# Products with the low parts of the weights moved to the end of each granule

## The chip, the cores and the metric

The kernel runs on one core of a Trainium2 chip. The metric is the device time of one execution in microseconds (us). A profile of one execution stands beside it: the span from the first to the last instruction, and what each engine did in it.

TensorE (PE in the profile) multiplies, VectorE is DVE, ScalarE is ACT, GpSimd is POOL, and SP is the queue that issues most transfers. Each engine works through its own queue in order and waits on semaphores where an operand comes from another engine.

## The reference, cut to what matters

One layer of a decoder trunk with 512 tokens and 2048 channels, all in float32:

```
h    = rmsnorm(x) * (1 + scale) + shift
proj = h @ w_in          # 2048 x 13632
q_lat, kv_lat, k_rope, z_mla, u, v, z_sgu, g_mla, g_sgu = split(proj)
y_mla  = causal_attention(q_lat, kv_lat, k_rope) * silu(z_mla)
y_sgu  = u * (tril(w_spatial) @ rmsnorm(v) + b_spatial) * silu(z_sgu)
merged = sigmoid(g_mla) * y_mla + sigmoid(g_sgu) * y_sgu
out    = rmsnorm(x + gate * (merged @ w_out))
```

The change lies in the projection `h @ w_in`, which takes the greater part of the time.

## The kernel before, in words

**Products in three parts.** A float32 operand is split into a high part (a cast to fp32r) and a low part (the rest). A product of two such operands is three matmuls added up in one PSUM bank: high by high, high by low, low by high. `mm3` (L156 to L159) issues these three in a row.

**Granules.** Weights arrive in granules of 128 rows and up to 1024 columns. For each granule ACT casts the high part (`w0h`, `w1h`, `Xh`), and DVE subtracts it from the raw tile to give the low part (`w0l`, `w1l`, `Xl`). The low part is therefore always ready after the high part. Which of the tiles a granule uses goes in turns: two pairs (`w0`, `w1`) in the stages before the blocks, three (`w1`, `w0`, `X`) in the blocks. A cast into a pair must wait until TensorE has read the high part of the granule that had the pair before, and a subtraction until it has read the low part.

**Stages.** The first stage (L440 to L464) projects 1024 columns into eight banks. The second stage (`ps2`, L524 to L536) projects 640 columns into five banks `ps2`: sixteen granules `g2[j]`, each of five `mm3`, 15 matmuls of 512 tokens. The plain stage (L704 to L732) has sixteen granules `gb[st]` and five banks `plain[0..4]` in the same way; in the granules 2, 5, 8, 11, 14 and 15 it adds matmuls for the rotary key (L720, L721). Beside its matmuls TensorE's neighbours have other work there: DVE sums the modulation weights, corrects `hh` and `hl` (the parts of h), and makes the sums of h's quarters; `lat_out` (L512) copies the five finished banks out on ACT at the start of the plain stage, and `evac_plain` (L622, L626) does so for `plain`.

**Blocks.** The remaining columns are done in eleven blocks of seven quarter products (a Strassen-like scheme), each block in 28 granules and each granule in 12 matmuls (L1440 to L1450): for each of two rows of channels `k` and two token halves `t` (bank `ps[t]`), the three parts of a product. 11 x 28 x 12 = 3696 matmuls. In the blocks the weights are the moving operand. Around the matmuls of granule s the lists of events run in a fixed order on ACT and DVE (`run(s, FIRST, HIGH, EVAC, GATE, SPLIT, BACK)`): HIGH casts the high part for granule s+2, EVAC copies out or combines banks that the granule before has finished, SPLIT makes the low part for granule s+2.

**After the blocks.** The attention projections (`mm_low_last`, L1541 to L1552) and the output projection (`out_granule`, L1749 to L1764) already issue all matmuls with the high part of the weights first and those with the low part last.

The order within every queue is as written in the program (`manual_schedule`); nothing reorders it.

Of the kernel before, what the change touches and what calls it, by code (L numbers as in the profile page):

```python
# [20 lines left out]
P = 128  # L21
D = 2048
S = 512
KC = D // P
# [113 lines left out]
def trunk_layer(ctx, tc, xT, xn, c, vecs, pos, wada, w1, w2, wv, wv3, wv4, wh, wh15, wq, wqr, wk, wvv, wo, wsT, bsp, gfin, out,  # L138
                dbg=None):
    nc = tc.nc  # L140
    ACT, DVE, PE, DMA = nc.scalar, nc.vector, nc.tensor, nc.sync
    LEFT, RIGHT = "left", "right"

    def tt(out, in0, in1, op):
        DVE.tensor_tensor(out=out, in0=in0, in1=in1, op=op)  # L145
# [10 lines left out]
    def mm3(ps, ah, al, bh, bl, start, stop):  # L156
        PE.matmul(ps, ah, bh, start=start, stop=False)  # L157
        PE.matmul(ps, ah, bl, start=False, stop=False)  # L158
        PE.matmul(ps, al, bh, start=False, stop=stop)  # L159
# [18 lines left out]
    def nt(p, shape, dt, tag, **kw):  # L178
        uid[0] += 1
        return p.tile(shape, dt, tag=tag, name=f"{tag}_{uid[0]}", **kw)  # L180
# [152 lines left out]
    def get(i, ahead=1, run=1):  # L333
        r = ws.get(i, ahead)
        fs, pend[:] = pend[:run], pend[run:]
        for f in fs:
            f()
        return r
# [8 lines left out]
    def bank_at(k):  # L347
        return nt(psp.p, [P, S], F32, f"ps{k}")

    def bank():  # L350
        n_bank[0] += 1
        return bank_at(ring[(n_bank[0] - 1) % len(ring)])
# [54 lines left out]
    hh, hl = [None] * KC, [None] * KC  # L407
# [21 lines left out]
    for q in range(4):  # L429
        for r in range(per):  # L430
            sl = slice(r * (S // per), (r + 1) * (S // per))
# [10 lines left out]
    for j in range(KC):  # L442
# [4 lines left out]
        wH, wL = get(g1[j], ahead=0)  # L447
# [11 lines left out]
        cols = [slice(m * P, (m + 1) * P) for m in range(8)]  # L459
# [6 lines left out]
                mm3(ps1[m], wH[:, cols[m]], wL[:, cols[m]], hh[j], hl[j], False, j == KC - 1)  # L466
    tt(ssx, ssx, sq, ALU.add)

    n_dot = 0

    def dot_to(n):
        nonlocal n_dot
        while n_dot < min(n, KC):
            ada_dot(n_dot)
            n_dot += 1
# [3 lines left out]
    def fix_begin(s_):  # L479
        if s_ in FIX_AT:  # L480
            j0 = n_fix
            assert n_dot >= j0 + 2
            tt(shift[:, j0:j0 + 2], dots[:, j0:j0 + 2], vec[:, C_BADA + j0:C_BADA + j0 + 2], ALU.add)
            tt(tw, xw[j0 // 2], rx.unsqueeze(1).broadcast_to([P, 2, S]), ALU.mult)

    def fix_end(s_):

        nonlocal n_fix
        if s_ in FIX_AT:
            js = low_at[s_ + 1] = range(n_fix, n_fix + 2)  # L490
# [12 lines left out]
    def store(dst, src):  # L503
        made.append((dst, src))

    def stores(n=None):
        for dst, src in leaving[:n]:
            DMA.dma_start(dst, src)
        leaving[:], made[:] = (leaving[n:] if n else []) + made, []
# [13 lines left out]
    ps2 = [bank() for _ in range(5)]  # L523
    for j in range(KC):  # L524
        fix_begin(j)
        wH, wL = get(g2[j])
        for m in range(5):
            sl = slice(m * P, (m + 1) * P)
            mm3(ps2[m], wH[:, sl], wL[:, sl], hh[j], hl[j], j == 0, j == KC - 1)
        if j < NB:  # L530
            DVE.reciprocal(out=rx[:, j * P:(j + 1) * P], in_=rx[:, j * P:(j + 1) * P])
        fix_end(j)
        dot_to(DOTS[j])
        if j == NB - 1:
            store(rx_d, rx)
        if j >= NB - 1:  # L536
            stores(1)
# [164 lines left out]
    plain = []  # L702
    for st in range(KC):
        fix_begin(KC + st)  # L704
        if st == 0:
            for f in pend:
                f()
            pend.clear()
        wH, wL = get(gb[st], ahead=0 if st == KC - 1 else 1)
        fix_end(KC + st)  # L710
        if KC + st < len(DOTS):
            dot_to(DOTS[KC + st])
        if st == 0:
            plain += [bank_at(k) for k in (3, 4, 5, 6, 7, 0)]
        for m in range(5):
            sl = slice(m * P, (m + 1) * P)
            mm3(plain[m], wH[:, sl], wL[:, sl], hh[st], hl[st], st == 0, st == KC - 1)
        for i, k in enumerate(rope_in.get(st, ())):
            both = wH[:, (5 + i) * P:(6 + i) * P]
            PE.matmul(plain[5], both, hh[k], start=k == 0, stop=False)  # L720
            PE.matmul(plain[5], both, hl[k], start=False, stop=k == KC - 1)  # L721
        if st == SUMS_AT:
            assert n_fix == KC
            ada.close()
            s12 = Scope("s12")
            for n in ("s2", "s1"):
                sums[n] = nt(s12.p, [P, 8, 2, 256], F32R, n)
            tb = Scope("tB")
        for f in early.pop(st, ()):
            f()  # L730
        stores(1)
# [547 lines left out]
    for group in (((10, "lat8"), (11, "lat9")), ((12, "lat10"), ("plain", "sinT"))):  # L1279
# [9 lines left out]
        i = group[0][0]  # L1289
# [126 lines left out]
    for b in range(len(BLOCKS)):  # L1416
        if b == 1:
            ring[:], n_bank[0] = [5, 6], 0
        for g, (p, i) in enumerate(V7):
            s = done[0] = at_block[b] + g  # L1420
            n = 1 if b or g else 2
            for f in pend[:n]:
                f()
            del pend[:n]
            for f in early.pop(KC + g, ()):
                f()
            if (b, g) == (1, 4):
                assert not pend and not early
                tb.close()
                mis = Scope("more")  # L1430
                sg[0] = Scope("sgu")
            if (b, g) == (1, 6):
                wide.clear()
            if g == 0 and b:
                v7["y_before"] = v7["y"]
            run(s, FIRST, HIGH, EVAC, GATE, SPLIT, BACK)
            if i == 0 and p in (1, 5, 6):
                which, banks = {1: ("y", y_of[b % 2]), 6: ("z", z_of), 5: ("w", z_of if b else (5, 6))}[p]
                v7[which] = [bank_at(k) for k in banks]
            ps = v7["y" if p < 5 else "z" if p > 5 else "w"]  # L1440
            wH, wL = (w.rearrange("p (k h w) -> p k h w" if BLOCKS[b][0] == "v" else "p (h k w) -> p k h w", h=4, k=2)
                      for w in vparts.pop((b, g)))
            for k in range(2):
                xh, xl = rights[p](2 * i + k)
                st, sp = i == k == 0 and p in (1, 5, 6), i == 3 and k == 1
                for t in range(2):
                    tk = slice(t * P, (t + 1) * P)
                    PE.matmul(ps[t].rearrange("p (h w) -> p h w", h=4), xh[:, tk], wH[:, k], start=st, stop=False, skip_group_check=True)  # L1448
                    PE.matmul(ps[t].rearrange("p (h w) -> p h w", h=4), xl[:, tk], wH[:, k], start=False, stop=False, skip_group_check=True)  # L1449
                    PE.matmul(ps[t].rearrange("p (h w) -> p h w", h=4), xh[:, tk], wL[:, k], start=False, stop=sp, skip_group_check=True)  # L1450
            run(s, MISC, LOAD)
            stores()
    v7["y_before"] = v7["y"]
# [133 lines left out]
    def kproj(h, ahead=1):  # L1587
        wH, wL = get(gk[h], ahead)
        ps = bank()
        mm_low_last(ps, wH, wL, range(6, 10))  # L1590
        return ps
# [154 lines left out]
    ps = kproj(0, 0)  # L1746
# [114 lines left out]
    for cg, k in ((2, 1), (3, 4)):  # L1861
        st = chunk_at[4 * cg + 3] + 1
# [21 lines left out]
    for cg in range(4):  # L1884
        for n in range(NB):
            cols = slice(cg * S, (cg + 1) * S)
# [131 lines left out]
```

## Time and profile before

| what | value |
|---|---|
| median of 3 runs | 1542.17 us (1541.4 to 1545.81) |
| the profiled execution: its time | 1543.22 us |
| the profiled execution: its span | 1541.3 us |
| PE busy | 1524.6 us, 99% of the span, 7152 matmuls |
| DVE busy | 1234.3 us, 80% |
| ACT busy | 806.6 us, 52% |
| POOL busy | 169.2 us, 11% |
| DMA, mean | 219 GB/s |
| granted TensorE clock, mean | 0.997 |

The time is 1.9 us more than the span, for what lies around it. A matmul that is shown with 0.39 us is pipelined: what counts for the rate is the distance from one start to the next, about 0.227 us for 512 columns. TensorE has waited where that distance is longer, and the bracket at the end of such a row names what ended the wait.

### The profile page before, as it was taken

The numbers are of one execution on the slowest core, as the hardware profiler recorded it, in microseconds if no ns is written. First come the engines' busy times: TensorE is split into PE (matmuls) and PEld (weight loads), VectorE is DVE, ScalarE is ACT, GpSimd is POOL, SyncE is SP. The second block draws the span as 40 slices with busy tenths as digits, with TensorE's granted clock in tenths as the row PEclk, the third lists the DMA queues.
The fourth block names the chain that finished last, engine by engine and source line by source line (L and its number), as shares of the span: only waits on it lengthen the run. The fifth ranks groups of instructions, "written<-read, shape, count | busy, mean of one in ns | idle before, by whom it ended". The sixth has DMA issues, their size and how long they took to land.

```text
span 1541.3 us, 20555 instructions
## 1 busy us (share of the span) xinstructions
PE 1524.6 (99%) x7152; PEld 1273.6 (83%) x7152; DVE 1234.3 (80%) x1676; ACT 806.6 (52%) x1276; POOL 169.2 (11%) x161
## 2 busy tenths in 40 slices
PE   9999999999999999999999999999999999999997
PEld 7888878888888887888888888888788888888886
DVE  8989897768787888887888787878689889965753
ACT  4445555546555546454555555556666666532331
POOL 0000000101000000011010100000122223221120
PEclk9999999999999999999999999999999999999999
DMA  9979775858886786878776866777788877759732
GB/s 377 388 269 347 237 220 164 233 148 241 245 223 184 214 227 199 226 214 212 206 200 186 223 205 190 236 193 215 193 205 195 203 185 193 194 148 338 283 103 110
DMA packets 368922, 337.93 MB, mean 219 GB/s; under 512 B 133689, under 2 KB 313969, under 8 KB 363697
## 3 DMA queue, kind: packets, MB, share of 16 engines
q1 hardware_dynamic: 345906, 313.54, 65.3%
q0 software_dynamic: 22912, 23.07, 9.7%
q8 instruction: 56, 0.92, 0.2%
q14 instruction: 48, 0.39, 0.1%
HBM read 302.38 MB, written 34.17 MB: 218 GB/s over the span
## 4 chain that ended last, share of the span: by engine, by line
PE 90%; DVE 4%; DMA 2%; SPq 2%; ACT 1%; issue 1%; ACTq 0%; DVEq 0%
PE ps L1448 17%; PE ps L1450 17%; PE ps L1449 17%; PE ps L463 5%; PE ps L158 5%; PE ps L159 5%; PE ps L157 5%; PE ps L1761 3%; PE ps L1763 3%; PE ps L1764 3%; PE ps L1549 3%; PE ps L1550 2%; PE ps L1552 2%; PE ps L1632 1%; SPq L102 1%
## 5 line engine op out<-in xcount | busy, mean ns | idle before, releaser
L145 DVE TENSOR_TENSOR X<-X,X 128x1024 fp32r<-128x1024 f32 (+2 forms) x111 | 130.4, 1182 | 28.8 <-ACT X L688 27.3
L688 ACT CAST X<-X 128x1024 fp32r<-128x1024 f32 x70 | 73.7, 1053 | 96.4 <-PE ps L1449 58.9
L688 ACT CAST w0h<-X 128x1024 fp32r<-128x1024 f32 x70 | 73.7, 1053 | 95.2 <-PE ps L1449 47.0
L688 ACT CAST w1h<-X 128x1024 fp32r<-128x1024 f32 x69 | 72.6, 1052 | 80.0 <-PE ps L1449 41.6
L145 DVE TENSOR_TENSOR w0l<-X,w0h 128x1024 fp32r<-128x1024 f32 x70 | 85.5, 1221 | 30.5 <-ACT w0h L688 28.9
L145 DVE TENSOR_TENSOR w1l<-X,w1h 128x1024 fp32r<-128x1024 f32 x69 | 84.2, 1221 | 25.7 <-ACT w1h L688 25.7
L122 DVE TENSOR_TENSOR w0l<-wraw,w0h 128x1024 fp32r<-128x1024 f32 (+3 forms) x61 | 65.7, 1078 | 36.3 <-ACT w0h L121 20.4
L145 DVE TENSOR_TENSOR X<-wraw,X 128x1024 f32<-128x1024 f32 (+1 forms) x65 | 79.3, 1221 | 16.9 <-ACT X L688 15.1
L122 DVE TENSOR_TENSOR w1l<-wraw,w1h 128x1024 fp32r<-128x1024 f32 (+3 forms) x60 | 69.9, 1165 | 28.6 <-ACT w1h L121 21.1
L1450 PE MATMUL ps<-w0l,hh 128*128 128x512 f32 x236 | 92.0, 390 | 0.4 <-DVE w0l L145 0.4
L1449 PE MATMUL ps<-w0h,hl 128*128 128x512 f32 x236 | 91.9, 389 | 0.0
L1450 PE MATMUL ps<-w1l,hh 128*128 128x512 f32 x236 | 91.8, 389 | 0.0
L1449 PE MATMUL ps<-w1h,hl 128*128 128x512 f32 x236 | 91.8, 389 | 0.0
L1448 PE MATMUL ps<-w0h,hh 128*128 128x512 f32 x236 | 91.8, 389 | 0.0
L1448 PE MATMUL ps<-w1h,hh 128*128 128x512 f32 x236 | 91.8, 389 | 0.0
L121 ACT CAST w0h<-wraw 128x1024 fp32r<-128x1024 f32 (+3 forms) x61 | 52.8, 866 | 73.1 <-PE ps L1764 20.4
L1450 PE MATMUL ps<-X,hh 128*128 128x512 f32 x232 | 90.6, 391 | 0.4 <-DVE X L145 0.4
L1448 PE MATMUL ps<-X,hh 128*128 128x512 f32 x232 | 90.4, 390 | 0.0
L1449 PE MATMUL ps<-X,hl 128*128 128x512 f32 x232 | 90.3, 389 | 0.0
L148 DVE SCALAR_TENSOR_TENSOR wada<-wada,cact 128x2048 f32<-128x2048 f32 x39 | 88.9, 2281 | 0.7 <-DMA wada<-in_wada 0.7
L121 ACT CAST w1h<-wraw 128x1024 fp32r<-128x1024 f32 (+3 forms) x60 | 52.6, 877 | 61.9 <-PE ps L158 20.1
L145 DVE TENSOR_TENSOR wraw<-wraw,X 128x1024 f32<-128x1024 f32 x66 | 80.4, 1218 | 0.6 <-DMA X<-in_wh 0.6
(462 smaller groups left out, 4404.2 us busy)
## 6 DMA issues: line engine op xcount, KB each, us to landing
X<-in_wh SPq DMA_DIRECT2D x131, 512.0 KB, 5.2
wada<-in_wada SPq DMA_DIRECT2D x39, 1024.0 KB, 7.6
wraw<-in_wo SPq DMA_DIRECT2D x32, 512.0 KB, 4.5
wraw<-in_wh SPq DMA_DIRECT2D x21, 512.0 KB, 5.1
wraw<-in_wh POOLq DMA_DIRECT2D x21, 512.0 KB, 7.7
turned<-p_d SPq DMA_DIRECT2D x64, 160.0 KB, 3.9
X<-in_wv SPq DMA_DIRECT2D x17, 512.0 KB, 4.1
X<-in_wh SPq DMA_DIRECT2D x22, 384.0 KB, 5.3
```

Source lines behind the costliest of these rows:

```text
L121: self.nc.scalar.copy(hi[:, :n], raw[:, :n])
L122: self.nc.vector.tensor_tensor(out=lo[:, :n], in0=raw[:, :n], in1=hi[:, :n].bitcast(F32), op=ALU.subtract)
L145: DVE.tensor_tensor(out=out, in0=in0, in1=in1, op=op)
L148: DVE.scalar_tensor_tensor(out=out, in0=in0, scalar=scalar, in1=in1, op0=op0, op1=op1, **kw)
L157: PE.matmul(ps, ah, bh, start=start, stop=False)
L158: PE.matmul(ps, ah, bl, start=False, stop=False)
L159: PE.matmul(ps, al, bh, start=False, stop=stop)
L463: PE.matmul(ps1[m], a[:, cols[m]], b, start=(j == 0 and a is wH and b is hh[j]), stop=False)
L688: ACT.copy(hi, t)
L1448: PE.matmul(ps[t].rearrange("p (h w) -> p h w", h=4), xh[:, tk], wH[:, k], start=st, stop=False, skip_group_check=True)
L1449: PE.matmul(ps[t].rearrange("p (h w) -> p h w", h=4), xl[:, tk], wH[:, k], start=False, stop=False, skip_group_check=True)
L1450: PE.matmul(ps[t].rearrange("p (h w) -> p h w", h=4), xh[:, tk], wL[:, k], start=False, stop=sp, skip_group_check=True)
```

## The change

A new function `low_last` issues for one granule first the two matmuls with the high part of the weights for every bank, and then the one with the low part for every bank. The second and the plain stage call it in place of five `mm3`. In the blocks the loop over k and t runs twice, first for the high part and then for the low part. Number, size and operands of the matmuls stay the same.

```
+    def low_last(banks, wH, wL, k):
+        cols = [slice(m * P, (m + 1) * P) for m in range(len(banks))]
+        for m, ps in enumerate(banks):
+            PE.matmul(ps, wH[:, cols[m]], hh[k], start=k == 0, stop=False)
+            PE.matmul(ps, wH[:, cols[m]], hl[k], start=False, stop=False)
+        for m, ps in enumerate(banks):
+            PE.matmul(ps, wL[:, cols[m]], hh[k], start=False, stop=k == KC - 1)
...
-        for m in range(5):
-            sl = slice(m * P, (m + 1) * P)
-            mm3(ps2[m], wH[:, sl], wL[:, sl], hh[j], hl[j], j == 0, j == KC - 1)
+        low_last(ps2, wH, wL, j)
...
-            mm3(plain[m], wH[:, sl], wL[:, sl], hh[st], hl[st], st == 0, st == KC - 1)
+        low_last(plain[:5], wH, wL, st)
...
+            for low in (False, True):
+                for k in range(2):
...
+                        if low:
+                            PE.matmul(to, xh[:, tk], wL[:, k], start=False, stop=sp, skip_group_check=True)
+                        else:
+                            PE.matmul(to, xh[:, tk], wH[:, k], start=st, stop=False, skip_group_check=True)
+                            PE.matmul(to, xl[:, tk], wH[:, k], start=False, stop=False, skip_group_check=True)
```

In the rows below a name is a tile with its running numbers: `ps` a bank, `w0h`/`w0l` and `w1h`/`w1l` the high and low part of a granule, `hh`/`hl` those of h. On PE, the last rows of the plain stage's granule 11 ahead of its rotary matmuls, before:

```order
L158 MATMUL ps_144_1470<-hl_138_1391,w1h_1593 128x512
L159 MATMUL ps_144_1470<-hh_135_1360,w1l_1594 128x512
L157 MATMUL ps_145_1471<-hh_135_1360,w1h_1593 128x512
L158 MATMUL ps_145_1471<-hl_138_1391,w1h_1593 128x512
L159 MATMUL ps_145_1471<-hh_135_1360,w1l_1594 128x512
L157 MATMUL ps_146_1472<-hh_135_1360,w1h_1593 128x512
L158 MATMUL ps_146_1472<-hl_138_1391,w1h_1593 128x512
L159 MATMUL ps_146_1472<-hh_135_1360,w1l_1594 128x512
```

The same rows of PE's queue now:

```order
L472 MATMUL ps_145_1471<-hh_135_1360,w1h_1593 128x512
L473 MATMUL ps_145_1471<-hl_138_1391,w1h_1593 128x512
L472 MATMUL ps_146_1472<-hh_135_1360,w1h_1593 128x512
L473 MATMUL ps_146_1472<-hl_138_1391,w1h_1593 128x512
L475 MATMUL ps_142_1468<-hh_135_1360,w1l_1594 128x512
L475 MATMUL ps_143_1469<-hh_135_1360,w1l_1594 128x512
L475 MATMUL ps_144_1470<-hh_135_1360,w1l_1594 128x512
L475 MATMUL ps_145_1471<-hh_135_1360,w1l_1594 128x512
L475 MATMUL ps_146_1472<-hh_135_1360,w1l_1594 128x512
```

The first use of `w1l` moved from the 3rd to the 11th matmul of the granule, the last use of `w1h` for the five banks from the 14th to the 10th (the rotary matmuls behind them still read it), and the bank `ps_142` is finished by the 11th instead of the 3rd.

On PE, the first eleven matmuls of the first block's granule 4 (counted from 0), with the waits that they carry, before:

```order
L1448 MATMUL ps_190_2035<-w0h_2081,hh_134_1357 128x512 [waits Activation_49]
L1449 MATMUL ps_190_2035<-w0h_2081,hl_137_1389 128x512
L1450 MATMUL ps_190_2035<-w0l_2082,hh_134_1357 128x512 [waits DVE_49]
L1448 MATMUL ps_191_2036<-w0h_2081,hh_134_1357 128x512
L1449 MATMUL ps_191_2036<-w0h_2081,hl_137_1389 128x512
L1450 MATMUL ps_191_2036<-w0l_2082,hh_134_1357 128x512
L1448 MATMUL ps_190_2035<-w0h_2081,hh_135_1360 128x512
L1449 MATMUL ps_190_2035<-w0h_2081,hl_138_1391 128x512
L1450 MATMUL ps_190_2035<-w0l_2082,hh_135_1360 128x512
L1448 MATMUL ps_191_2036<-w0h_2081,hh_135_1360 128x512
L1449 MATMUL ps_191_2036<-w0h_2081,hl_138_1391 128x512
```

The same eleven matmuls' places now:

```order
L1457 MATMUL ps_190_2035<-w0h_2081,hh_134_1357 128x512 [waits Activation_49]
L1458 MATMUL ps_190_2035<-w0h_2081,hl_137_1389 128x512
L1457 MATMUL ps_191_2036<-w0h_2081,hh_134_1357 128x512
L1458 MATMUL ps_191_2036<-w0h_2081,hl_137_1389 128x512
L1457 MATMUL ps_190_2035<-w0h_2081,hh_135_1360 128x512
L1458 MATMUL ps_190_2035<-w0h_2081,hl_138_1391 128x512
L1457 MATMUL ps_191_2036<-w0h_2081,hh_135_1360 128x512
L1458 MATMUL ps_191_2036<-w0h_2081,hl_138_1391 128x512
L1455 MATMUL ps_190_2035<-w0l_2082,hh_134_1357 128x512 [waits DVE_49]
L1455 MATMUL ps_191_2036<-w0l_2082,hh_134_1357 128x512
L1455 MATMUL ps_190_2035<-w0l_2082,hh_135_1360 128x512
```

The wait for DVE's low part moved from the 3rd to the 9th matmul. The high part is read for the last time by the 8th instead of the 11th, and the bank of the first token half is finished by the 11th instead of the 9th.

On ACT, two casts and the copies of the two banks behind them in a later block (`d` is the tile that holds a copied quarter), before:

```order
L688 CAST w1h_2759<-X_250_2443 128x1024 [waits DMASW4_49,DMASW5_49,PE_49,Activation_49]
L688 CAST w0h_2781<-X_289_2660 128x1024 [waits DMAHW5_49,DMAHW6_49,DVE_49,PE_49]
L906 COPY d_310_2784<-ps_282_2623 128x512
L906 COPY d_310_2784<-ps_283_2624 128x512 [waits PE_49]
L688 CAST X_311_2800<-wraw_260_2491 128x1024 [waits DMASW6_49,DMASW7_49,DVE_49,PE_49]
```

The same rows now:

```order
L694 CAST w1h_2759<-X_250_2443 128x1024 [waits DMASW4_49,DMASW5_49,PE_49,Activation_49]
L694 CAST w0h_2781<-X_289_2660 128x1024 [waits DMAHW5_49,DMAHW6_49,DVE_49,PE_49]
L910 COPY d_310_2784<-ps_282_2623 128x512 [waits PE_49]
L910 COPY d_310_2784<-ps_283_2624 128x512 [waits PE_49]
L694 CAST X_311_2800<-wraw_260_2491 128x1024 [waits DMASW6_49,DMASW7_49,DVE_49,PE_49]
```

The queue is in the same order; the copy of the first bank has a wait for PE of its own, since the wait of the cast ahead of it no longer covers the bank's last matmul. There are 43 such copies on ACT. The queues of DVE, POOL and SP are the same as before, with the same engines waited for.

More of the change, by code (lines that the diff above doesn't have):

```diff
@@ L714, in trunk_layer @@
             plain += [bank_at(k) for k in (3, 4, 5, 6, 7, 0)]
-        for m in range(5):
-            sl = slice(m * P, (m + 1) * P)
-            mm3(plain[m], wH[:, sl], wL[:, sl], hh[st], hl[st], st == 0, st == KC - 1)
+        low_last(plain[:5], wH, wL, st)
         for i, k in enumerate(rope_in.get(st, ())):
@@ L1442, in trunk_layer @@
                       for w in vparts.pop((b, g)))
[L1443 to L1450, printed above, removed]
+            for low in (False, True):
+                for k in range(2):
+                    xh, xl = rights[p](2 * i + k)
+                    st, sp = i == k == 0 and p in (1, 5, 6), i == 3 and k == 1
+                    for t in range(2):
+                        tk = slice(t * P, (t + 1) * P)
+                        to = ps[t].rearrange("p (h w) -> p h w", h=4)
+                        if low:
[3 more added lines that the diff above has]
+                            PE.matmul(to, xl[:, tk], wH[:, k], start=False, stop=False, skip_group_check=True)
             run(s, MISC, LOAD)
```

## The prediction

> **What bounds the kernel now.** I read the page's engine totals, the chain that ended last, the stages, and then every distance between two starts of matmuls, since a busy share of 99% does not tell how often TensorE waits.
>
> ```profile
> PE 1524.6 (99%) x7152; PEld 1273.6 (83%) x7152; DVE 1234.3 (80%) x1676; ACT 806.6 (52%) x1276; POOL 169.2 (11%) x161
> PE 90%; DVE 4%; DMA 2%; SPq 2%; ACT 1%; issue 1%; ACTq 0%; DVEq 0%
> 98.00:152.00 54.00, 54.00 (x239) 44.50 (x237) 46.86 (x55) 23.44 (x34) 0.00 (x0) 1.00 0.94 346
> 152.00:217.00 65.00, 63.48 (x278) 51.65 (x277) 56.57 (x95) 34.95 (x56) 0.00 (x0) 1.00 0.76 236
> 217.00:1075.00 858.00, 856.85 (x3780) 705.74 (x3779) 698.68 (x795) 471.53 (x612) 68.01 (x56) 1.00 0.75 208
> 1345.00:1492.00 147.00, 147.00 (x689) 123.12 (x688) 92.72 (x114) 46.39 (x73) 27.57 (x22) 1.00 0.70 231
> ```
>
> The rows by stage give the stretch, its length, and the busy time of PE, PEld, DVE, ACT and POOL, then the granted clock. PE's idle time is 0.00 us in the second stage, 65.00 - 63.48 = 1.52 in the plain stage, and 858.00 - 856.85 = 1.15 in the eleven blocks. An order of matmuls can win only what TensorE waits in these 977 us, some 3 us.
>
> Does the order itself have a price? Two granules of a block (old order) and the starts of two output granules (high first, low last):
>
> ```profile
> 700.43 0.39 PE L1448 MATMUL ps<-w1h,hh 128*128 128x512 f32 x1
> 703.15 0.39 PE L1448 MATMUL ps<-w0h,s 128*128 128x512 f32 x1
> 1409.99 1.81 PE ps L1761 x8
> 1415.43 1.81 PE ps L1761 x8
> ```
>
> Old: (703.15 - 700.43) / 12 = 0.2267 us from start to start. New pattern: (1415.43 - 1409.99) / 24 = 0.2267 us. The 480 reordered matmuls of the two stages and the 3696 of the blocks cost the same either way, at a granted clock of 1.00 in both stages' rows.
>
> **The change part by part.** *1. The waits for the low part go.* These are the places where the third matmul of a granule came late (its row behind the second's):
>
> ```profile
> 187.81 0.39 PE L158 MATMUL ps<-hl,w1h 128*128 128x512 f32 x1
> 188.47 0.50 PE L159 MATMUL ps<-hh,w1l 128*128 128x512 f32 x1 [0.27 <-DVE w1l L122]
> 195.44 0.39 PE L158 MATMUL ps<-hl,w1h 128*128 128x512 f32 x1
> 197.08 0.50 PE L159 MATMUL ps<-hh,w1l 128*128 128x512 f32 x1 [1.25 <-DVE w1l L122]
> 222.60 0.39 PE L1449 MATMUL ps<-X,hl 128*128 128x512 f32 x1
> 222.95 0.50 PE L1450 MATMUL ps<-X,hh 128*128 128x512 f32 x1
> 228.30 0.39 PE L1449 MATMUL ps<-w0h,hl 128*128 128x512 f32 x1
> 229.06 0.50 PE L1450 MATMUL ps<-w0l,hh 128*128 128x512 f32 x1 [0.37 <-DVE w0l L145]
> 579.78 0.40 PE L1449 MATMUL ps<-X,hl 128*128 128x512 f32 x1
> 580.60 0.50 PE L1450 MATMUL ps<-X,hh 128*128 128x512 f32 x1 [0.43 <-DVE X L145]
> ```
>
> Distance less 0.2267: 0.43, 1.41, 0.12, 0.53 and 0.59 us, 3.08 in all. In the plain stage the low part is now read by the 11th matmul, 8 x 0.2267 = 1.81 us later than the 3rd; in a block by the 9th, 6 x 0.2267 = 1.36 us later. Each single wait is shorter than that, so each by itself would vanish.
>
> *2. But their sum is not won whole.* The first two give TensorE a lead of 0.43 + 1.41 = 1.84 us at the end of the plain stage, and there DVE and ACT are late by themselves:
>
> ```profile
> 217.25 1.05 ACT L688 CAST w0h<-X 128x1024 fp32r<-128x1024 f32 x1 [1.18 <-DVE X L145]
> 219.65 0.39 PE L1448 MATMUL ps<-w0h,s 128*128 128x512 f32 x1
> 220.59 1.05 ACT L688 CAST X<-X 128x1024 fp32r<-128x1024 f32 x1
> 222.37 0.39 PE L1448 MATMUL ps<-X,hh 128*128 128x512 f32 x1
> 227.79 1.21 DVE L145 TENSOR_TENSOR w0l<-X,w0h 128x1024 fp32r<-128x1024 f32 x1
> 228.07 0.39 PE L1448 MATMUL ps<-w0h,hh 128*128 128x512 f32 x1
> ```
>
> The first matmul of a granule needs the high cast as before, and the change moves nothing there. Granule 1's cast ends at 217.25 + 1.05 = 218.30, released by a sum on DVE and not by TensorE: the lead is cut to 219.65 - 218.30 = 1.35. Granule 2's cast is queued on ACT behind that one and ends at 221.64: the lead is 222.37 - 221.64 = 0.73. There the 0.12 wait goes too (0.85). With the few matmuls that followed a wait at 0.24 apart back at 0.2267 it is about 0.95 at granule 4, which starts at 227.1. Its low part is ready at 227.79 + 1.21 = 229.00, and its 9th matmul is due at 227.1 + 1.81 = 228.9: a rest of about 0.1 us stays of the 0.53. Four matmuls later the granule ends near 229.95, before at 229.06 + 10 x 0.2267 = 231.33 (231.48 with its slower starts): lead about 1.5 us. That is my term for the first four waits; its ends are 0.73 (the smallest lead met) and 2.49 (all four).
>
> *3. The wait at 580* then gives 0.59 more, if its cast moves with TensorE:
>
> ```profile
> 574.35 1.06 ACT w0h L688
> 578.24 1.05 ACT L688 CAST X<-X 128x1024 fp32r<-128x1024 f32 x1 [2.84 <-DVE X L145]
> ```
>
> The high part ends at 579.29, only 0.26 us ahead of its first use at 579.55 (0.2267 before the row at 579.78). The chain of waits goes back from it, over DVE, to the cast at 574.35, which follows TensorE's release of a high part; so it should move with the lead. Sum 2.1 us, ends 0.99 and 3.08.
>
> *4. High parts come free earlier.* The last read of a high part moves from the 11th to the 8th matmul of a block granule (0.68 us) and from the 14th to the 10th in the two stages (0.91), except where rotary matmuls follow.
>
> ```profile
> ACT X L688 <- PE ps L1449: 78.5, 60, 2.6
> ACT w1h L688 <- PE ps L1449: 64.9, 48, 2.6
> ACT w0h L688 <- PE ps L1449: 58.9, 42, 2.3
> 1075.16 0.84 ACT L121 CAST w0h<-wraw 128x768 fp32r<-128x768 f32 x1 [1.88 <-PE ps L1449]
> 1086.95 0.50 PE L1630 MATMUL ps<-d,d 128*128 128x512 f32 x1 [0.73 <-ACT d L162]
> 1089.14 0.73 PE L1632 MATMUL ps<-hh,hl 128*128 128x512 f32 x1 [0.81 <-DVE hl L145]
> ```
>
> These 150 waits of casts (202 us) are hidden by TensorE's work: shortening them wins nothing while TensorE has its operands. One may count: the cast at 1075.16 waits for the last block's high part and starts the dense run on ACT and DVE that ends in the attention's first two waits. It may start up to 0.68 earlier; between 0 and 0.68 I take 0.3, since the bank copies behind it (next step) give a part back.
>
> *5. Banks are finished closer together and later.* In a block the first half's bank is ready two matmuls (0.45 us) later, the second half's as before, and 43 copies on ACT have a wait of their own. Before, such a pair stood so:
>
> ```profile
> 703.17 1.06 ACT L688 CAST w1h<-X 128x1024 fp32r<-128x1024 f32 x1 [1.14 <-issue]
> 704.13 1.06 ACT L906 COPY d<-ps 128x512 f32<-128x512 f32 x2
> ```
>
> The granule ended at 703.15. Its 11th matmul would start at 702.70 and, at 0.39 long, end at 703.09; the cast ahead of the copy is done a full 1 us after that, and 0.3 us after it even if it starts 0.68 earlier. Cost 0; without that cover 0.45 a pair. DVE's combinations of banks start up to 0.45 later, ahead of low parts that are now needed 1.36 later: 0 as well.
>
> At the end of the second stage the five banks are copied out while the plain stage starts:
>
> ```profile
> 150.38 2.63 ACT L512 COPY d<-ps 128x512 f32<-128x512 f32 x4 [0.17 <-PE ps L159]
> 153.10 0.59 ACT L512 COPY lat<-ps 128x512 f32<-128x512 f32 x1
> 153.59 0.73 ACT L121 CAST w1h<-wraw 128x640 fp32r<-128x640 f32 x1
> 156.31 0.39 PE L157 MATMUL ps<-hh,w1h 128*128 128x512 f32 x1
> ```
>
> The first bank is ready eight matmuls later, so the copies start at 150.38 + 1.81 = 152.19. Five at 0.49 (153.59 - 153.10) to 0.66 (2.63 / 4) end at 154.6 to 155.5, the cast behind them at 155.4 to 156.2; its high part is needed at 156.31. Cost 0, with 0.1 to 0.9 us to spare.
>
> *Sum.* 1.5 + 0.6 + 0.3 = 2.4 us. The profiled execution's span would go from 1541.3 to 1538.9, its time from 1543.22 to 1540.8; it lies 1.05 above the median, so the median goes from 1542.17 to about 1539.8 (-0.16%). A measurement tells about 0.3% (4.6 us) from no change.
>
> **The rivals.** *A, the lead is eaten by high casts.* DVE has 56.57 of 65.00 us in the plain stage, and if the cast at 578.24 does not move, TensorE keeps 0.26 of lead there and 0.59 is regained: about 0.9, 1541.3 us. For it speak the 1.18 and 2.84 us that casts wait on DVE, against it the 150 waits on TensorE itself.
>
> *B, nothing is won*: 1542.2. The plain stage's DMA and DVE chains would have to set even the blocks' pace; DVE's 81% there (698.68 / 858) speaks against it.
>
> *C, all is won*: 3.08 + 0.68, and the two attention waits (0.73 + 0.81) go whole: 5.3 us, 1536.9.
>
> *D, slower.* The later bank holds ACT. If in each of the 43 pairs the copy came to its wait before the 11th matmul is done and TensorE waited for what is behind it, 43 x 0.45 = 19.5 us, 1561.7. It decides where the cast ahead ends less than 0.06 us ahead of the granule's end; at 704.13 it was a microsecond after.
>
> *E, a lower clock*, since the low matmuls now change banks every time. The output rows above change banks every time (L1761 and its neighbours) at clock 1.00, which speaks against it. Were 5% lost over 4176 x 0.2267 = 947 us, it would be 47 us: 1589. The Trainium skill ("TensorE: Matmul & The Clock Gate", section "A second HAM failure mode: psum-queue depth-cycling") says that cycling through banks at 512 columns can make TensorE pause so often that its clock gate swings; by that rule this rival would come true, and the trace's 0.2267 in both orders disagrees with it here.
>
> **How the numbers follow.** Forecast 0.60; A 0.20; B 0.06; C 0.07; D 0.05; E 0.02. A and B lie within 0.3%, as the forecast does: same 0.86; faster 0.07 (C); slower 0.07 (D, E). The range takes in the term's upper ends, 3.08 + 0.68 = 3.8 and up to 1.5 more from the attention's waits (1536.9), and at the top B with the scatter of a median (the best two of the runs shown are 0.8 apart): 1543.3.
>
> **What would show it.** Right: no waits for a low part at the five places; granule 2 of the first block starting on its cast's heels near 221.7 us; the block stage still 2.72 us a granule; attention's first scores some 2 to 3 us earlier. Wrong: distances of more than 0.23 between matmuls in the blocks, waits of a first matmul on a cast after 230 us, or an ACT copy that holds the casts behind it.

## The result, and the profile after

| kernel | median, us | lowest to highest | runs |
|---|---|---|---|
| before | 1543.38 | 1541.4 to 1545.81 | 8 |
| after | 1538.51 | 1537.24 to 1539.73 | 8 |

The ratio is 0.9968, with a 95% interval of 0.9957 to 0.9979: the change makes the kernel 4.9 us faster (3.2 to 6.6), about twice the 2.4 us that were forecast. The three runs of before that stood ahead of the prediction have a lower median (1542.17) than all the later sets of before (1543.08 to 1543.74), so a difference counts here and not a time by itself. The profiled execution of after took 1538.12 us, with a span of 1536.2.

First the engine totals, the chain that ended last, and three stages, in the same columns as before:

```profile
PE 1521.3 (99%) x7152; PEld 1272.9 (83%) x7152; DVE 1233.6 (80%) x1676; ACT 804.9 (52%) x1276; POOL 169.2 (11%) x161
PE 92%; DVE 3%; DMA 2%; SPq 1%; ACT 1%; issue 1%; DVEq 0%; ACTq 0%
98.00:152.00 54.00, 54.00 (x238) 44.36 (x237) 47.37 (x55) 22.67 (x32) 0.00 (x0) 1.00 0.96 350
152.00:217.00 65.00, 64.72 (x285) 53.06 (x284) 55.96 (x94) 35.78 (x58) 0.00 (x0) 1.00 0.77 235
217.00:1072.00 855.00, 854.36 (x3775) 705.21 (x3775) 699.80 (x796) 471.30 (x614) 68.02 (x56) 1.00 0.75 209
```

The work is the same: 7152 matmuls, and no engine's busy time moved by more than 3.3 us. TensorE (PE) is idle for 0.28 us instead of 1.52 in the plain stage, and for 0.64 instead of 1.15 in the blocks. DVE's share of the chain fell from 4% to 3%.

The chain of waits, cut to a stretch in the middle of the blocks (560 to 800 us), says more. Before:

```profile
by line: PE ps L1448 26.5%; PE ps L1449 26.5%; PE ps L1450 26.3%; issue 2.5%; DVE d L145 2.2%; DMA half<-in_wh 2.0%; DMA t_d<-d 1.7%; DVE w1l L145 1.5%; DVE X L145 1.5%; PE ps L158 1.0%; DVE wraw L145 0.9%; ACT w1h L688 0.9%; ACT w0h L688 0
```

And after:

```profile
by line: PE ps L1458 32.5%; PE ps L1457 32.5%; PE ps L1455 32.3%; PE ps L159 0.9%; PE ps L158 0.8%; PE ps L157 0.8%; PE ps L1103 0.4%
```

Before, the chain left TensorE in this stretch and ran over DVE, ACT and transfers; after, these rows of TensorE make up all but rounding. So the blocks did have places where TensorE waited for others, and more of them than the one at 580.

To see where the time came from I compared the start of the same matmul in both profiles (+ is earlier after the change):

| place | after's lead, us | won since the row above |
|---|---|---|
| first granule of the second stage (98 us) | -0.82 | the start-up differs by this between the two executions |
| plain stage, granule 12 | +0.80 | 1.62 |
| block 0, granule 2 | -0.32 | -1.12 |
| block 0, granule 10 | +0.30 | 0.62 |
| block 10, first granule | +2.91 | 2.61 |
| attention, first scores' first matmul (`d` by `d`, L1630) | +2.91 | 0 |
| first matmul behind these scores (L1549, a projection) | +5.13 | 2.22 |
| end | +4.93 | -0.20 |

The two terms that the prediction had far too small are the blocks behind block 0 (2.61 for 0.59) and the attention's start (2.22 for 0.3).

*The blocks.* The missing waits are those of the spatial mixing, three matmuls (`mm3`, L157 to L159) that are laid between granules. Its low operand `vl` is made by DVE. One of its six places, before (TensorE's rows, DVE's and ACT's, by start):

```profile
767.33 1.03 ACT L688 CAST w0h<-wraw 128x1024 fp32r<-128x1024 f32 x1
768.40 1.22 DVE L145 TENSOR_TENSOR w0l<-wraw,w0h 128x1024 fp32r<-128x1024 f32 x1 [2.67 <-ACT w0h L688]
...
775.94 0.69 DVE L145 TENSOR_TENSOR vl<-lat,sinT 128x512 fp32r<-128x512 f32 x1
776.08 0.39 PE L157 MATMUL ps<-sinT,whl 128*128 128x512 f32 x1
776.68 0.50 PE L158 MATMUL ps<-vl,whl 128*128 128x512 f32 x1 [0.21 <-DVE vl L145]
```

And after:

```profile
765.96 1.23 DVE L145 TENSOR_TENSOR w0l<-wraw,w0h 128x1024 fp32r<-128x1024 f32 x1 [2.67 <-ACT w0h L694]
...
773.50 0.69 DVE L145 TENSOR_TENSOR vl<-lat,sinT 128x512 fp32r<-128x512 f32 x1
774.12 0.39 PE L157 MATMUL ps<-sinT,whl 128*128 128x512 f32 x1
774.35 0.40 PE L158 MATMUL ps<-vl,whl 128*128 128x512 f32 x1
```

`vl` starts 7.54 us after the subtraction `w0l` in both, and DVE is without a gap between them: nothing in DVE's queue waits but that subtraction, for ACT's cast. Here the cast stands behind other work in ACT's queue, and the way back to TensorE is long. It is short at the place at 583 us, where the run of operations on ACT and DVE that ends in `vl` begins with a cast that TensorE released. Before:

```profile
568.21 0.39 PE L1449 MATMUL ps<-w1h,s 128*128 128x512 f32 x1
568.68 1.05 ACT L688 CAST w1h<-X 128x1024 fp32r<-128x1024 f32 x1 [1.67 <-PE ps L1449]
```

And after:

```profile
566.95 0.39 PE L1458 MATMUL ps<-w1h,s 128*128 128x512 f32 x1
567.42 1.05 ACT L694 CAST w1h<-X 128x1024 fp32r<-128x1024 f32 x1 [1.67 <-PE ps L1458]
```

The matmul that releases the cast is the 11th of its granule before and the 8th after, and the cast starts 0.47 us behind it in both; `vl` comes 14.11 us behind this cast before (at 582.79) and 13.84 after (at 581.26). So what changed is where this train of operations stands against TensorE: at 776, `vl` starts 0.14 us ahead of the first mixing matmul before, and 0.62 ahead of it after. The second matmul follows the first at 0.60 us before and at 0.23 after. The six places cost 0.19, 0.41, 0.11, 0.48, 0.20 and 0.11 us before, 1.5 in all; after, one of 0.19 is left. Of the 2.61 us, then, 0.7 are the wait at 580 with the slow distance behind it, 1.3 the mixing, and the rest of 0.6 the matmuls behind these waits, of which many follow each other at 0.23 to 0.24 us instead of 0.2267.

*The attention's start.* The rows of TensorE there, after:

```profile
1084.04 0.50 PE L1638 MATMUL ps<-d,d 128*128 128x512 f32 x1 [0.73 <-ACT d L162]
1084.38 0.39 PE L1639 MATMUL ps<-d,d 128*128 128x512 f32 x1
1085.56 0.50 PE L1640 MATMUL ps<-hh,hl 128*128 128x512 f32 x1 [0.79 <-DVE hl L145]
1085.90 0.40 PE L1641 MATMUL ps<-hl,hl 128*128 128x512 f32 x1
```

and the further rows of before, with the stretch behind them in the stage view (before, then after):

```profile
1087.83 0.51 PE L1631 MATMUL ps<-d,d 128*128 128x512 f32 x1 [0.38 <-DVE d L145]
1089.67 0.63 PE L1633 MATMUL ps<-hl,hl 128*128 128x512 f32 x1
1090.10 0.63 PE L1634 MATMUL ps<-d,d 128*128 128x512 f32 x1
1089.00:1092.70 3.70, 3.56 (x11) 3.27 (x12) 2.99 (x7) 1.61 (x2) 0.00 (x0) 0.54 0.29 112
```

```profile
1089.00:1092.70 3.70, 3.70 (x18) 3.04 (x17) 3.23 (x10) 2.67 (x9) 0.00 (x0) 1.00 0.00 0
```

The two waits that the prediction listed are still there (0.73 and 0.79). A third one between them, for `d` on DVE, went: 1087.83 - 1086.95 = 0.88 us before and 0.34 after. From the first of the three waiting matmuls to the last it is 1089.14 - 1086.95 = 2.19 before and 1085.56 - 1084.04 = 1.52 after, 0.67 won. The rest, 2.22 - 0.67 = 1.55 us, is not a wait. Before, the granted clock's mean over these 3.70 us is 0.54, and two matmuls of 512 columns stand 0.43 apart; after it is 1.00. The record of the clock has one stretch at 0.5 there, 3.41 us long. Whether it comes is not a matter of the waits alone (last section).

### The profile page after: what moved, and what is told of

Same layout as the page of the kernel before. It is cut to its first block, busy times and chain, and to the rows that moved or that the text cites. A ratio compares the mean times of both kernels' runs of the same rounds, so it can differ in the third digit from the quotient of the medians.

```text
span 1536.2 us, 20578 instructions
## 1 busy us (share of the span) xinstructions
PE 1521.3 (99%) x7152; PEld 1272.9 (83%) x7152; DVE 1233.6 (80%) x1676; ACT 804.9 (52%) x1276; POOL 169.2 (11%) x161
## 4 chain that ended last, share of the span: by engine, by line
PE 92%; DVE 3%; DMA 2%; SPq 1%; ACT 1%; issue 1%; DVEq 0%; ACTq 0%
PE ps L1457 18%; PE ps L1458 18%; PE ps L1455 18%; PE ps L463 5%; PE ps L158 3%; PE ps L1769 3%; PE ps L1771 3%; PE ps L1772 3%; PE ps L159 3%; PE ps L157 3%; PE ps L1557 3%; PE ps L1558 2%; PE ps L1560 2%; PE ps L472 2%; PE ps L473 2%; PE ps L475 1%
## 5 line engine op out<-in xcount | busy, mean ns | idle before, releaser
L1457 PE MATMUL ps<-X,hh 128*128 128x512 f32 x232 | 90.5, 390 | 0.3 <-ACT X L694 0.3
L659 POOL DMA_DIRECT2D X<-in_wh x9 | 11.6, 1284 | 536.9 <-DVE w1l L145 178.8
L1702 POOL TENSOR_TENSOR hl<-turned,hh 128x384 fp32r<-128x384 f32 (+1 forms) x48 | 45.9, 984 | 222.1 <-ACT hh L1701 156.4
L145 DVE TENSOR_TENSOR d<-ps,d 128x512 fp32r<-128x512 f32 (+1 forms) x90 | 58.8, 682 | 8.2 <-ACT d L162 8.2
```

Of the source, the lines that this page charges most:

```text
L1457: PE.matmul(to, xh[:, tk], wH[:, k], start=st, stop=False, skip_group_check=True)
```

## The experiments

Three causes were to be told apart: *late lows* (the low part is read later in the granule), *early release* (the high part is read to its end earlier, and with it the casts and the train on DVE behind them move), and *the clock* (the shorter waits at the attention's start spare the half clock). The first four take the change apart by stage and by part. All kernels but the last are timed in five rounds, each against before on the same chip.

**The plain stage alone** (`e1_plain_only`).

```
 plain stage:   - mm3(plain[m], ...) for five banks
                + low_last(plain[:5], wH, wL, st)
 second stage, blocks: as before
```

> Only the plain stage issues its low matmuls last; second stage and blocks as before. Theory T (the measured gain is the waits for low parts, plus waits elsewhere that shrink because casts run earlier): the lead won in the plain stage is 1.6 us at the first block, but the low waits in the first block's granules 2 and 4 stay and grow by what the lead adds, so that after granule 5 at most 0.6 us of it is left; span about 0.5 us shorter. Rival R (only the lateness of each low part counts, leads just add up): 1.6 us shorter. If the half clock at the start of the attention is a matter of chance, either can come with 1.5 us more or less, to be read from the clock events of the profile.

Measured 1543.41 us against 1543.08, ratio 1.0006 (0.9997 to 1.0014): nothing. The lead is +1.08 us at the plain stage's granule 12, counted from the start-up, and -0.68 by block 0's granule 5. There it ran into the parts as they come from ACT and DVE (TensorE, in block 0):

```profile
219.71 0.50 PE L1454 MATMUL ps<-w0h,s 128*128 128x512 f32 x1 [0.32 <-ACT w0h L696]
220.97 0.50 PE L1456 MATMUL ps<-w0l,s 128*128 128x512 f32 x1 [0.53 <-DVE w0l L145]
224.30 0.50 PE L1456 MATMUL ps<-X,hh 128*128 128x512 f32 x1 [0.35 <-DVE X L145]
230.40 0.50 PE L1456 MATMUL ps<-w0l,hh 128*128 128x512 f32 x1 [0.36 <-DVE w0l L145]
```

A lead that comes into this stretch is lost in it. This profile also has a wait for a low part at the blocks' end (0.95 us at 1072.39) that before's profile does not have, so the list of late low parts differs from one execution to another.

**The blocks alone** (`e2_blocks_only`).

```
 blocks:        + for low in (False, True):  around the loops over k and t
 second stage, plain stage: as before
```

> Only the blocks issue their low matmuls last. Theory T: the two waits of the plain stage (0.44 and 1.41 us) stay, all of the blocks' gain stays: the low waits at 222, 228 and 580 us and nearly all waits of the spatial mixing matmuls (1.5 us in the profile before) go, and the blocks end about 3 us earlier relative to the first block; with the attention's 0.7 about 3.5 us, 5 where the half clock at the attention's start is gone too. Rival R: 1.4 us, with the mixing matmuls' waits as before.

Measured 1538.73 us against 1543.08, ratio 0.9971 (0.9962 to 0.9981): as much as the whole change. The two low-part waits of the plain stage are still there (0.95 and 1.43 us in this profile), and none is left in the blocks.

**The blocks in two halves.** The next two take a table for the order of a block granule's twelve matmuls, in place of the loops; each entry is k, t and a part, with 0 for `xh` by the high part, 1 for `xl` by the high part, 2 for `xh` by the low part. `e3_early_free` reads the low part third, as before, but has read the high part to its end by the 9th matmul:

```
+ EARLY_FREE = [(0,0,0),(0,0,1),(0,0,2),(0,1,0),(0,1,1),(1,0,0),(1,0,1),(1,1,0),(1,1,1),(0,1,2),(1,0,2),(1,1,2)]
- for k in range(2): ... for t in range(2):
+ for k, t, part in EARLY_FREE:
```

> Blocks only, half of the change: the first low matmul stays the 3rd of its granule, the other three go to the end. So the low part is awaited as early as before, but the high part comes free after the 9th instead of the 11th matmul. Theory T (casts and with them DVE run earlier): the waits of the mixing matmuls shrink from 1.5 to under 0.6 us and the wait at 580 us by about 0.4; the low waits at 222 and 228 us stay; blocks about 1.3 us shorter. Rival R (late low parts alone): no gain, within 0.3 us.

Measured 1540.53 us against 1543.08, ratio 0.9983 (0.9975 to 0.9992). In block 0 nothing is won (the wait at 230 stays), and 2.06 us of lead in the blocks behind it. The mixing at 776, in this kernel:

```profile
775.76 0.68 DVE L145 TENSOR_TENSOR vl<-lat,sinT 128x512 fp32r<-128x512 f32 x1
776.20 0.39 PE L157 MATMUL ps<-sinT,whl 128*128 128x512 f32 x1
776.50 0.50 PE L158 MATMUL ps<-vl,whl 128*128 128x512 f32 x1
```

`vl` now starts 0.44 us ahead of the first matmul, with the low part read third as before: the release alone moved it. The wait at 580, which I had put down to late lows, shrank to 0.11 here, since the low part comes earlier as well.

`e4_late_low` does the other half: the low part is first read by the 8th matmul, but the last high product comes twelfth, one matmul later than before.

```
+ LATE_LOW = [(0,0,0),(0,0,1),(0,1,0),(0,1,1),(1,0,0),(1,0,1),(1,1,0),(0,0,2),(0,1,2),(1,0,2),(1,1,2),(1,1,1)]
+ for k, t, part in LATE_LOW:
```

> Blocks only, the other half: the low part is first read by the 8th matmul, but one matmul with the high part is put last, so that the high part comes free only after the 12th. Theory T: the low waits at 222, 228 and 580 us go (1.4 us), but the waits of the mixing matmuls stay at 1.5 us or grow to 2.5, since TensorE runs ahead of a DVE that is not earlier: blocks 0 to 1 us shorter. Rival R: the same gain as with all low matmuls last, 3 us.

Measured 1542.74 us against 1543.08, ratio 0.9999 (0.999 to 1.0008): nothing. No wait for a low part is left in the blocks, and 0.95 us is won in block 0; the blocks behind it lose 0.91 again, at the mixing:

```profile
583.81 0.50 PE L158 MATMUL ps<-vl,whl 128*128 128x512 f32 x1 [0.82 <-DVE vl L145]
776.34 0.39 PE L157 MATMUL ps<-sinT,whl 128*128 128x512 f32 x1
776.70 0.68 DVE L145 TENSOR_TENSOR vl<-lat,sinT 128x512 fp32r<-128x512 f32 x1
777.44 0.50 PE L158 MATMUL ps<-vl,whl 128*128 128x512 f32 x1 [0.71 <-DVE vl L145]
```

`vl` starts 0.36 us behind the first matmul, and the six places cost 3.6 us instead of 1.5. This kernel is not late lows in purity, since its release is 0.23 us later than before; that is a part of the 0.50 by which `vl` fell back. What it shows is that taking the low waits away wins nothing when the high part is freed later. Late lows with the release of before, at the 11th matmul, were not run.

How far `vl` moves can be read at the mixing steps where it has more room. At the one at 847 us it starts this much ahead of the first mixing matmul:

| kernel | last read of the high part by | `vl` ahead, us | moved, us |
|---|---|---|---|
| before | 11th matmul | 0.49 | |
| after | 8th | 1.17 | +0.68 |
| `e3_early_free` | 9th | 0.94 | +0.45 |
| `e4_late_low` | 12th | 0.26 | -0.23 |

These are three, two and minus one distances of 0.2267 us, as many as the last read moved; at the steps at 469, 490 and 819 us they are the same within 0.02 us. When the low part is first read (by the 9th, the 3rd and the 8th matmul) leaves no mark on them.

**The mixing a granule later, in before** (`e5_mix_later`): if `vl` comes too late, its reader may come later.

```
-        on(s_, MISC, sgu_mix, g)
+        on(s_ + 1, MISC, sgu_mix, g)
-            out_at[g] = place(max(s_ + 1, ready["u", c, half] + 1), 0.46, sgu_out, g, half)
+            out_at[g] = place(max(s_ + 2, ready["u", c, half] + 1), 0.46, sgu_out, g, half)
```

> The kernel before, with the three matmuls of each spatial mixing step issued one granule later; nothing else of the order is changed. If what the freed casts won lies in the waits of these matmuls for the split of v (theory T), then the waits at 540, 583, 612, 776, 819 and 848 us (1.5 us in all) go here too, without any high part coming free earlier, and the time is 1 to 1.5 us shorter, with the wait at 580 us as before. Rival: the waits are those of a DVE that is late for everything; then they come back elsewhere in the blocks (a low part late by the same amount) and nothing is won.

Measured 1546.73 us against 1543.26, ratio 1.0022 (1.0013 to 1.0031): slower. In the blocks the mixing waits are gone and the lead grows by 1.32 us from block 0 to block 10, close to their 1.5. But the last steps of the mixing come a granule later too, and 4.0 us are lost at the blocks' end and at the first projection behind them (TensorE):

```profile
1064.60 0.50 PE L1448 MATMUL ps<-w0h,hh 128*128 128x512 f32 x1 [0.40 <-ACT w0h L688]
1065.86 0.50 PE L1450 MATMUL ps<-w0l,hh 128*128 128x512 f32 x1 [0.53 <-DVE w0l L145]
1078.92 0.50 PE L1549 MATMUL ps<-hh,w1h 128*128 128x512 f32 x1 [1.92 <-ACT w1h L121]
```

So the mixing waits are real and worth what the rows say, and this is a poor way to spare them.

**The clock, first attempt** (`e6_before_filled`, and `e7_after_filled` with the same edit in after): 38 small matmuls are added to keep TensorE busy in the waits of the first scores. They write to the score banks ahead of the products, which start those banks anew.

```
+ def fill_in(ps, n):
+     w = ident[:, 0:P // 2].bitcast(BF16)
+     for _ in range(n): PE.matmul(ps[:, :P], w, w, start=True, stop=True)
  ahead of three of the first scores' matmuls: fill_in(s3, 14), fill_in(s1, 8), fill_in(s1, 16)
```

> The kernel before, with 38 small bf16 matmuls (no part of the result) in the three waits ahead of the first scores of the attention. Theory: TensorE's idle 2.6 us there lets the granted clock fall to one half for 3.4 us in some executions (the profile before has such an event, that after has none), 1.55 us each time. Filled, no execution has it: the profile has no half clock ahead of the end, and the median is 0.4 to 0.8 us shorter, since not every execution of the kernel before has the event. Rival: the event does not come from the waits; it stays and the time is the same or 0.3 us longer.

> The changed kernel with the same 38 small matmuls. Its waits there are shorter (1.9 us) and its profile has no half clock, so nothing is left to win: within 0.3 us of the changed kernel (1538.5), 4.5 us ahead of the kernel before. If the changed kernel has the event in some executions, up to 0.5 us better.

Measured 1545.23 us against 1543.26 in before (ratio 1.0012, 1.0004 to 1.0021), and 1540.48 in after (0.9983, 0.9974 to 0.9992), 2 us slower than without them. The attempt missed: it changed another engine's waits. ACT's first rows of the softmax, in before and then with the added matmuls:

```profile
1089.35 1.28 ACT L1660 ACT_TABLE_LOAD   x1
1093.49 0.69 ACT L1660 ACTIVATE d<-ps,mx 128x512 f32<-128x512 f32 x1 [2.86 <-DVE mx L152]
```

```profile
1094.11 1.28 ACT L1668 ACT_TABLE_LOAD   x1 [3.49 <-DVE mx L152]
1095.40 0.69 ACT L1668 ACTIVATE d<-ps,mx 128x512 f32<-128x512 f32 x1
...
1115.68 0.50 PE L1549 MATMUL ps<-hh,w0h 128*128 128x512 f32 x1 [2.37 <-ACT w0h L121]
```

With one more writer of the score bank the activation waits for TensorE as well; its wait for DVE's maximum then stands on the table load ahead of it, in the program as built. The load of 1.28 us, which lay under that wait before, now follows it; ACT runs late, and TensorE waits 2.37 us at 1115.68, where before it waited 0.54. The half clock did go at 1089, and came back behind this new wait (at 1116.2, and at 1111.9 in `e7_after_filled`).

**The clock, second attempt** (`e9_before_filled_own_bank`, `e10_after_filled_own_bank`): the same matmuls write to a bank that nothing reads then.

```
+ spare = bank_at(0) if h == 0 and i == 3 else None
  fill_in(spare, 14), fill_in(spare, 8), fill_in(spare, 16) at the same places
```

> As the first filled kernel, but the 38 small matmuls write a bank of their own, so that no other engine has to wait for them and the load of the exponential's table on ACT starts as early as in the kernel before. Theory: no half clock at 1089 us, 1.55 us won at the first scores; up to 0.4 of it lost at the cast that the second head's projection waits for (near 1113 us); median 0.4 to 0.8 us shorter than the kernel before, since some of its executions have no half clock there. Rival: the half clock does not come from these waits or what it costs is taken back whole at 1113 us: the time is the same within 0.3 us.

> The changed kernel with the small matmuls in a bank of their own. If the changed kernel still has the half clock in some executions, 0.2 to 0.5 us shorter than the changed kernel (1538.5), else the same; in both cases 4.5 to 5 us ahead of the kernel before.

Measured 1542.99 us (before with them) against 1543.74, ratio 0.9995 (0.9986 to 1.0004), and 1538.54 (after with them), ratio 0.9968 (0.9955 to 0.998). Before with them, the stretch that had the half clock:

```profile
1089.00:1092.70 3.70, 3.70 (x36) 3.23 (x34) 3.57 (x7) 2.94 (x4) 0.00 (x0) 1.00 0.55 215
```

The clock is 1.00 in this stretch, the runs lie within 1.4 us (1542.26 to 1543.67) instead of 4.0 (1542.24 to 1546.27), and the median is 0.75 lower, which five rounds do not tell from nothing. After with them is as fast as after without (1538.51). Between these two kernels, with TensorE kept busy at that place in both, 1542.99 - 1538.54 = 4.45 us of the gain stand. So the half clock is a part of the profiled pair's difference, and at most a small part of the medians'.

**The second stage alone** (`e8_second_only`, three rounds): `low_last(ps2, wH, wL, j)`, all else as before.

> Only the second stage issues its low matmuls last. It had no wait before, so all theories say no change: within 0.3 us of the kernel before, but for the copies of its five banks, which all come at its end: if these delay the cast of the plain stage's second granule, up to 0.6 us are lost at its first matmul.

Measured 1542.98 us against 1543.26, ratio 0.9998 (0.9989 to 1.0007). No price, no gain. Its profile is of use for the clock: at the attention's start it has the three waits of before (0.89, 0.66 and 1.09 us) and no half clock, and from the first scores to the projection behind them it wins 1.53 us on before's profile. That is what the half clock costs, and the waits alone do not bring it.

## Why the prediction came out right in direction and half in size

*The bound (some 3 us in the three stages).* TensorE won 3.73 us there (from -0.82 to +2.91 in the table). The bound was read from idle time, and a matmul counts as busy for 0.39 us where the next could start after 0.2267, so up to 0.16 us of each wait does not show: the row at 222.95 has no bracket, at 0.35 us behind the one ahead of it.

*The price of the order (nothing).* As forecast. In after's blocks matmuls still follow each other at 0.2267 us at clock 1.00, and the second stage alone moves nothing. Rival E, the lower clock by the Trainium skill's psum-queue depth-cycling ("TensorE: Matmul & The Clock Gate"), did not come: the clock of 1.00 stands in all three stage rows above, with a bank change at every low matmul.

*Steps 1 and 2, the first four waits (1.5 us).* The mechanism held; the size was 1.12 (1.62 - 1.12 + 0.62, the first three differences of the table). The plain stage won 1.62 of the 1.84, with a new wait of 0.28 at 192.25 for a high part. One pair of profiles does not fix this size. The first of the plain stage's two waits, 0.43 in before's profile, was 0.95, 1.27 and 1.55 us in `e2_blocks_only`, `e3_early_free` and `e4_late_low`, whose plain stage is the same; and the whole term, 1.12 here, is 0.72 in `e10_after_filled_own_bank` and 0.05 in `e7_after_filled`. Then the lead was cut at granules 1 and 2 of block 0 by the casts that the prediction named (after):

```profile
192.25 0.50 PE L472 MATMUL ps<-hh,w0h 128*128 128x512 f32 x1 [0.28 <-ACT w0h L121]
218.26 1.05 ACT L694 CAST w0h<-X 128x1024 fp32r<-128x1024 f32 x1 [1.18 <-DVE X L145]
219.36 0.50 PE L1457 MATMUL ps<-w0h,s 128*128 128x512 f32 x1 [0.34 <-ACT w0h L694]
221.59 1.05 ACT L694 CAST X<-X 128x1024 fp32r<-128x1024 f32 x1
222.69 0.50 PE L1457 MATMUL ps<-X,hh 128*128 128x512 f32 x1 [0.30 <-ACT X L694]
```

Granule 2 should start "near 221.7" and started at 222.69, since the casts were 1 us later by the profile's clock than before (218.26 for 217.25), of which the later start of the second stage is 0.82. The plain stage's own contribution came to nothing: the blocks alone have all of the gain.

*Step 3, the wait at 580 (0.59).* Gone, as forecast, worth 0.59 and another 0.11 (below). But the reason that I gave, the later use, is one of two: the early release alone (`e3_early_free`) took 0.48 of it.

*Step 4, the high parts (0 in the blocks, 0.3 at the attention).* This is the step that failed. It said that "shortening them wins nothing while TensorE has its operands", and looked at the weights' operands alone. The casts' waits in after (total, times, longest, in us):

```profile
ACT X L694 <- PE ps L1458: 74.5, 57, 2.6
ACT w0h L694 <- PE ps L1458: 68.1, 47, 2.6
ACT w1h L694 <- PE ps L1458: 58.4, 43, 2.6
```

Their sum is 201 us, as before (202): the cast still waits for TensorE, only at an earlier point of the granule. What moved is all that ACT and DVE do behind it, and one of those tiles, `vl`, was late by 0.1 to 0.5 us at six places. I had listed the late *low parts of weights* and not, as the prediction says, every distance between two starts, so 1.5 us of waits never entered the sum. The early release alone is worth 2.06 us of lead and a ratio of 0.9983; late lows, with a release one matmul later than before, 0.9999; late lows and early release together 0.9971. At the attention the term was 0.67 us, the upper of its stated ends (0 and 0.68) and not the 0.3 taken.

*Step 5, the banks (0).* As forecast: the 43 copies on ACT hold up nothing that TensorE shows.

*Left out of the sum:* the mixing (1.3 us won), 0.11 us behind each wait that went and the slower starts after it, and the half clock (1.55 us in the profiled pair, less in the medians). By the rows above, 1.1 + 2.6 + 0.7 = 4.4 us without the clock. That this is so close to the 4.45 between the two filled kernels is in part luck, since the first term differs between executions; the 2.6 does not (2.61, 2.61, 2.64 and 2.55 against before's profile in the four kernels with the new order of the blocks). That the result lies in the prediction's range is in part luck too: its lower end was added up from other waits.

Of the rivals, C (all is won, 1536.9) is nearest beside the forecast, though for waits that it did not count; A was right on granules 1 and 2 and wrong at 580, where the cast did move with TensorE.

## What to carry to other kernels

When the last read of a buffer moves earlier, look beyond the wait of the cast that refills it: everything behind that cast in queues that run without gaps moves with it, and the tile that comes late may belong to another step. List every matmul that starts late, whatever its operand, before pricing a new order. And a lead that is won just ahead of a stretch where the producers themselves are late is lost in that stretch, so the plain stage's 1.8 us of waits were worth nothing and the blocks' smaller ones everything.

## What the runs showed of the hardware that was not expected

*Half clock after three short waits, in some executions.* Before, TensorE waited 0.89, 0.65 and 1.08 us (distances less 0.2267) within 3.1 us, 2.6 in all, and the clock was 0.5 for the next 3.41 us. The same three waits in `e8_second_only` left it at 1.00, while `e1_plain_only` and `e4_late_low` have the half clock again (from 1092.45 and 1091.15 us). What tells them apart is where the waits lie on a grid. In every profile the changes of the clock are a whole number of 3.413 us apart (443.73 us, for example, is 130 of them), and the first one comes 3.8 to 7.0 us behind the start of the span, so the grid is not tied to the kernel. I cut each profile into stretches of 3.413 us from that first change on and summed TensorE's waits in each stretch at full clock. Where they came to 2.1 us or more, the next stretch ran at 0.5; there are five such stretches (2.63 us before, 2.40 in `e4_late_low`, 2.10 in `e1_plain_only`, and 2.64 and 2.36 around one long wait in `e6_before_filled` and `e7_after_filled`). Where they came to 1.9 us or less, it never did (the most is 1.89, in `e2_blocks_only`). In `e8_second_only` a boundary cuts the third wait, and the fullest stretch has 1.79; after has 1.65.

The Trainium skill ("TensorE: Matmul & The Clock Gate", Part 1, on the HAM clock gate) states half speed after an idle window of about 3.4 us, with windows that run free of the kernel. The length of 3.413 us and the free grid agree with that; that 2.1 us of waits in a window are enough does not agree with a window that is idle throughout.

How often executions of before have the half clock was not measured, since only one of each kernel was profiled. If the grid falls anywhere with equal chance, before's waits put 1.9 to 2.1 us or more into one stretch in about half of the cases (44 to 56%), which at 1.53 us each would be 0.7 to 0.9 us on the average: an estimate from these rows. The 0.75 us between the medians of before without and with added matmuls, and the scatter that shrank from 4.0 to 1.4 us with them, are in keeping with it. After's waits could come to at most 2.07 us in one stretch, between the two bounds, so whether it ever has the half clock is not shown; that it is no faster with the added matmuls (1538.54 against 1538.51) speaks against it.

*A wait costs 0.11 us more than itself.* The first distance behind a wait is 0.34 us instead of 0.227 (1084.04 to 1084.38, 219.36 to 219.69, 776.68 to 777.02 in before).

*A table load can come out from under a wait.* One more engine to wait for put 1.28 us of loading on ACT's path (`e6_before_filled`), and about 2 us on the kernel's time.
